# Reciprocal roots of the latents in pairs, and three weight splits moved from GpSimd to VectorE

## The chip, the cores and the metric

The kernel runs on one core of one Trainium2 chip, in one launch. The metric is the device time of one execution in microseconds (us); the median of several runs is given. The engines are PE (TensorE: matmuls and transposes), DVE (VectorE), ACT (ScalarE), POOL (GpSimd) and SP (SyncE, which here only issues DMAs).

## What is computed

Two transformer blocks in a row on 256 tokens of width 1024, all in fp32. The change touches the first half of the first block, cut here to the parts that matter:

```python
mod = silu(c) @ w_ada + b_ada                   # six vectors: sh1, sc1, gt1, sh2, sc2, gt2
h  = rmsnorm(x, g_norm1) * (1 + sc1) + sh1      # 256 x 1024
hc = rmsnorm(ctx, g_norm1) * (1 + scc1) + shc1  # the context, 256 x 1024
cq, ckv, kpe, rq, rk, rv, rg = split(h @ w_in)  # widths 256, 256, 32, 4 x 512
cq_c, ckv_c, kpe_c, ...      = split(hc @ w_in)
q   = rmsnorm(cq, g_q) @ w_uq                   # 8 heads of 64 + 32, rope on the 32
k,v = rmsnorm(ckv, g_kv) @ w_ukv                # 8 heads of 64 + 64; keys get kpe, with rope
# the same for ckv_c, kpe_c without rope; keys and values of both are joined
o_mla = softmax(q k^T / sqrt(96)) v             # 8 heads, 256 queries, 512 keys
o = concat(o_mla, retention(rq, rk, rv, rg)) @ w_out
x = x + gt1 * o
```

A convolutional feed-forward layer, and a second block with windowed attention, a gated recurrence, cross-attention and a feed-forward layer, follow. `rmsnorm(x, g)` is `x * (mean(x*x) + 1e-6) ** -0.5 * g` over a row. The *latents* are the 256-wide `cq` (query latents), `ckv` (key/value latents) and `ckv_c` (context latents), each in two tiles of 128 tokens.

## The kernel before, in words

Tokens lie on the 128 partitions, in two tiles. A product in fp32 is made of three products in the matmul format fp32r (`mm3`, line 185): each factor is split into a high part (a rounded copy) and a low part (the factor less its high part), and high x high, high x low and low x high are summed in PSUM. So each block of weights, 128 x 1024 of `raw` that a DMA brought, is split before use in `Weights.unit`: ACT casts the high part `wh` (line 222), and a subtraction makes the low part `wl` (line 225). Where a gain is folded in, lines 229 and 230 (ACT and DVE) do the same. Tiles of activations are transposed by PE against an identity matrix into a PSUM tile `tr` (line 167), and split on the way out: ACT casts the high part (line 159), DVE subtracts (line 160). There are two `tr` buffers.

Line 225 runs on DVE, except that before the end of the first half of the first block every third split after the sixteenth goes to POOL:

```python
GPU = 3
GPN = 16
eng = nc.gpsimd if GPU and self.ext is None and self.cnt % GPU == 0 and self.cnt > GPN else nc.vector
```

There are three such splits.

The program is written as Python generators; a scheduler then sets the order of each engine's instructions by their dependences, their modelled costs and some priorities. An engine runs its instructions strictly in the order that comes out, and an instruction that waits holds up all behind it.

The stages around the change, in the order of time:

- *ada ticks* (lines 544 and 547, DVE): the modulation vectors are summed up from 128 x 1024 blocks of `w_ada`, a block at a time, in between other work. When a vector is complete, `ada_done` multiplies it with a matrix of ones on PE, into `tr` tiles (lines 520 and 526); for `gt1` DVE adds the two halves to the bias (line 522) just before the latents begin, and until then both `tr` buffers are held.
- *Latents* (lines 612 to 676). One product gives `cq`, `ckv`, `kpe` and the context's `ckv`, `kpe` in PSUM tiles (`acc` and `at`). For each of the two query latents: ACT copies it to SBUF (line 636), ACT squares and sums it (`mean_sq`, line 143), POOL adds epsilon and raises to -0.5 (lines 640 and 641), and it is transposed and split. Its root `rq` is applied later, to the products with `w_uq` (line 695). Then, for each of the four key/value and context latents: ACT's square, POOL's root (`finish_rstd`, lines 138 and 139), ACT's scaled copy (line 663), transposition and split, and rope on the 32 columns of `kpe` (`rope32`, lines 650 to 656, DVE) or a copy of them (line 668). So POOL computes six roots, 128 x 1 each, query latents first. Products of a further projection (`strand_d`, line 185 into `acc`) fill PE's time beside it.
- *Weave* of attention and the remaining projections. For each half of the queries and each of eight heads `mla_half` has PE compute scores (line 742), DVE their maximum (745, 746), ACT the exponential with its sum (748), DVE the reciprocal and the normalisation (749, 750), PE four transposes (753), DVE or ACT the copy out of PSUM (758, 756), and PE the product with the values (764). Projections' products, weight splits and ada ticks lie in between.

Of the kernel before, what the change touches and what calls it, by code (L numbers as in the profile page):

```python
# [9 lines left out]
F32 = mybir.dt.float32  # L10
# [3 lines left out]
AF = mybir.ActivationFunctionType  # L14
# [10 lines left out]
EPS = 1e-6  # L25
# [5 lines left out]
MLA_ACT = (2, 5)  # L31
MOD = 'VVAVVAVA'
MID = 1
GPU = 3
GPN = 16
START = 'mmaamxXmaammaammaamaamaakmaaacaC'
NT2 = 5
NS1 = 4
# [51 lines left out]
def _body(nc, tc, A, out, es):  # L90
# [24 lines left out]
    def small(w=1, tag="sm", bufs=None):  # L115
        kw = {} if bufs is None else {"bufs": bufs}
        return sm.tile([P, w], F32, tag=f"{tag}{w}", name=f"{tag}{w}", **kw)
# [24 lines left out]
    def mean_sq(a, n, ss):  # L142
        nc.scalar.activation(junk[:, 0:a.shape[-1]], a, AF.Square, scale=n ** -0.5, accum_out=ss)  # L143
# [44 lines left out]
    class Weights:  # L188
        def __init__(self, pl, nraw, nsplit):
            self.base, self.nraw, self.nsplit = pl, nraw, nsplit  # L190
            self.ext, self.next, self.n = None, 0, 0
            self.cnt = 0

        def extend(self, pl, nsplit):
            self.ext, self.next, self.n = pl, nsplit, 0
# [20 lines left out]
        def unit(self, ap, nk, width, gains=None, raw=None):  # L216
            n = nk * width
            if raw is None:
                raw = self.load(ap, nk, n)
            wh, wl = self.pair()  # L220
            if gains is None:
                nc.scalar.copy(wh[:, 0:n], raw[:, 0:n])  # L222
                self.cnt += 1
                eng = nc.gpsimd if GPU and self.ext is None and self.cnt % GPU == 0 and self.cnt > GPN else nc.vector
                eng.tensor_tensor(out=wl[:, 0:n], in0=raw[:, 0:n], in1=wh[:, 0:n].bitcast(F32), op=ALU.subtract)  # L225
            else:
                for k in range(nk):
                    s = slice(k * width, (k + 1) * width)
                    nc.scalar.activation(wh[:, s], raw[:, s], AF.Copy, scale=gains[k])  # L229
                    nc.vector.scalar_tensor_tensor(out=wl[:, s], in0=raw[:, s], scalar=gains[k],  # L230
                                                   in1=wh[:, s].bitcast(F32), op0=ALU.mult,
                                                   op1=ALU.subtract)
            return wh, wl
# [62 lines left out]
    with ExitStack() as e1:  # L296
# [334 lines left out]
        ckT_l = S4((P, 2, 512), F32R)  # L631
        rq_rs = []
        kpe = s.tile([P, 4, 32], F32, name="kpe")
        for t in range(2):
            cq = S1()
            nc.scalar.copy(cq, aq[t][:, 0:256])
            r = small(1, "rq", 2)
            ss = small(1, "ss")
            mean_sq(aq[t][:, 0:256], 256, ss)
            nc.gpsimd.tensor_scalar(out=r, in0=ss, scalar1=EPS, scalar2=None, op0=ALU.add)  # L640
            nc.gpsimd.tensor_tensor(out=r, in0=r, in1=mhalf[:, 0:1], op=ALU.pow)
            rq_rs.append(r)
            transpose_split(cq, cqT_h[:, :, t * P:(t + 1) * P], cqT_l[:, :, t * P:(t + 1) * P], 2)

        def rope32(dst, src, t, nh):
            cb = C1("mcos")[:, t * 32:(t + 1) * 32]
# [11 lines left out]
        fill(1)  # L658
        for i in range(4):
            a = akv[i] if i < 2 else akc[i - 2]  # L660
            r = rms(a[:, 0:256], 256)
            ck = S1()
            nc.scalar.activation(ck, a[:, 0:256], AF.Copy, scale=r)
            transpose_split(ck, ckT_h[:, :, i * P:(i + 1) * P], ckT_l[:, :, i * P:(i + 1) * P], 2)
            if i < 2:
                rope32(kpe[:, i:i + 1, :], a[:, 256:288].unsqueeze(1), i, 1)
            else:
                nc.vector.tensor_copy(kpe[:, i, :], a[:, 256:288])
        tt = tr_tile()
        for i in range(4):  # L670
            nc.tensor.transpose(tt[0:32, i * P:(i + 1) * P], kpe[:, i, :], ident)
# [878 lines left out]
```

## Time and profile before

| | |
|---|---|
| median of 3 runs | 844.55 us (844.31 to 845.6) |
| the profiled execution | 847.59 us, of which 845.8 us are the span from its first to its last instruction |
| PE busy | 811.1 us, 96% of the span |
| DVE busy | 618.4 us, 73% |
| ACT busy | 481.4 us, 57% |
| POOL busy | 50.5 us, 6%, in 85 instructions |
| granted TensorE clock, mean | 0.991 of full speed |

The span is one execution as the profiler saw it. An engine's busy time counts the time in which it executes; waiting is idle time. The granted clock is given as a share of 2.4 GHz: 1.00 is that, 0.50 is 1.2 GHz. In rows of the timeline the first number is the start from the span's beginning, the second the duration, both in us; then come engine, line, operation, output and inputs by their names in the program, shapes and the number of instructions in the row. In brackets stands the idle time of the engine before it, and the instruction whose end is taken to have released it.

### The profile page before, as it was taken

Reading aid. Unit: us, or ns where it says so; the run is one execution under the profiler, and the core shown is the slowest. Engines: PE = TensorE matmul, PEld = TensorE weight load, DVE = VectorE, ACT = ScalarE, POOL = GpSimd, SP = SyncE. Lnnn points to the kernel's source line nnn. Section 1 sums busy time; section 2 is a strip of 40 time slices with the busy share of each in tenths; the row PEclk is TensorE's granted clock in tenths of the full one; section 3 lists DMA queues with packets and bytes.
Section 4 is the critical chain, followed back from the end, with each engine's and each line's share of the span. In section 5 each row is a group of like instructions: output and inputs, shape, how many; then the busy total and the mean of one; then the engine's idle time right before and its main releaser. Section 6 shows DMA issues by size and latency. Waiting matters only on the chain.

```text
span 845.8 us, 11966 instructions
## 1 busy us (share of the span) xinstructions
PE 811.1 (96%) x4368; PEld 657.4 (78%) x4368; DVE 618.4 (73%) x1036; ACT 481.4 (57%) x850; POOL 50.5 (6%) x85
## 2 busy tenths in 40 slices
PE   5989989999999999999999999999999999999996
PEld 4856968667687888888887777777788788888885
DVE  5638969995797698878778656875747787867743
ACT  7337354333565686656656656665626876757631
POOL 0000020110110200000000400001001100000000
PEclk9988999999999999999999999999999999999999
DMA  9796878853154566666564453433633686666501
GB/s 336 273 351 237 261 286 297 303 186 132 50 180 133 179 218 220 182 193 192 184 199 150 126 150 129 146 110 118 195 101 97 176 250 188 186 197 184 193 1 50
DMA packets 81531, 155.20 MB, mean 183 GB/s; under 512 B 5184, under 2 KB 43584, under 8 KB 81472
## 3 DMA queue, kind: packets, MB, share of 16 engines
q1 hardware_dynamic: 81472, 154.44, 56.7%
q8 instruction: 34, 0.56, 0.3%
q14 instruction: 25, 0.20, 0.1%
HBM read 152.85 MB, written 1.05 MB: 182 GB/s over the span
## 4 chain that ended last, share of the span: by engine, by line
PE 68%; ACT 2%; POOL 2%; DVE 1%; issue 1%; POOLq 0%; DVEq 0%; ACTq 0%
PE acc L185 34%; PE tr L255 9%; PE at L255 7%; PE tr L258 4%; PE at L258 3%; ACT junk L143 1%; PE at L1317 1%; PE at L1295 1%; PE tr L167 1%; PE tr L1236 1%; PE at L1186 1%; PE at L1188 1%; PE at L1266 0%; PE tr L764 0%; PE at L793 0%
## 5 line engine op out<-in xcount | busy, mean ns | idle before, releaser
L185 PE MATMUL acc<-wh,xT 128*128 128x512 f32 (+2 forms) x544 | 169.2, 388 | 1.8 <-ACT xT L159 1.8
L222 ACT CAST wh<-raw 128x1024 fp32r<-128x1024 f32 (+1 forms) x90 | 91.0, 1013 | 86.0 <-PE acc L185 30.5
L225 DVE TENSOR_TENSOR wl<-raw,wh 128x1024 fp32r<-128x1024 f32 (+1 forms) x87 | 103.5, 1192 | 36.9 <-ACT wh L222 36.7
L185 PEld LDWEIGHTS acc<-wh,xT 128*128 128x128 f32 x544 | 99.0, 189 | 24.6 <-issue 3.6
L225 DVE TENSOR_TENSOR xl<-raw,xh 128x1024 fp32r<-128x1024 f32 x68 | 82.6, 1220 | 29.2 <-ACT xh L222 28.5
L185 PE MATMUL acc<-wl,xT 128*128 128x512 f32 (+2 forms) x272 | 97.9, 386 | 0.0
L229 ACT ACTIVATE wh<-raw,fm 128x256 fp32r<-128x256 f32 (+3 forms) x128 | 70.3, 605 | 41.4 <-DMA raw<-in_wv_x_dram 13.7
L185 PE MATMUL acc<-xh,xT 128*128 128x512 f32 x288 | 92.9, 398 | 0.0
L222 ACT CAST xh<-raw 128x1024 fp32r<-128x1024 f32 x68 | 71.0, 1048 | 36.5 <-PE acc L185 12.8
L230 DVE SCALAR_TENSOR_TENSOR wl<-raw,fm,wh 128x256 fp32r<-128x256 f32 (+3 forms) x128 | 71.7, 609 | 15.9 <-ACT wh L229 15.7
L185 PEld LDWEIGHTS acc<-xh,xT 128*128 128x128 f32 x288 | 53.4, 188 | 11.7 <-issue 0.8
L255 PE MATMUL tr<-xT,wh 128*128 128x512 f32 x192 | 61.2, 398 | 0.0
L185 PEld LDWEIGHTS acc<-wl,xT 128*128 128x128 f32 x272 | 50.4, 190 | 10.0 <-issue 2.2
L185 PE MATMUL acc<-xl,xT 128*128 128x512 f32 x144 | 53.1, 395 | 0.0
L230 DVE SCALAR_TENSOR_TENSOR xl<-raw,fm,xh 128x256 fp32r<-128x256 f32 (+2 forms) x76 | 38.0, 550 | 12.7 <-ACT xh L229 12.7
L229 ACT ACTIVATE xh<-raw,fm 128x256 fp32r<-128x256 f32 (+2 forms) x76 | 37.7, 559 | 16.8 <-PE acc L185 8.1
L185 PE MATMUL acc<-xh,g 128*128 128x512 f32 x160 | 44.1, 389 | 0.0
L258 PEld LDWEIGHTS tr<-xT,wl 128*128 128x128 f32 x192 | 36.1, 188 | 7.9
L255 PE MATMUL at<-xT,xh 128*128 128x512 f32 x128 | 40.2, 395 | 0.0
L255 PE MATMUL at<-xT,wh 128*128 128x512 f32 x128 | 40.2, 395 | 0.0
L255 PE MATMUL tr<-xT,xh 128*128 128x512 f32 x128 | 40.2, 395 | 0.0
L258 PE MATMUL tr<-xT,wl 128*128 128x256 f32 x192 | 38.6, 278 | 0.0
(365 smaller groups left out, 1567.9 us busy)
## 6 DMA issues: line engine op xcount, KB each, us to landing
raw<-in_w_up_dram SPq DMA_DIRECT2D x66, 512.0 KB, 4.0
raw<-in_w_ada_dram SPq DMA_DIRECT2D x48, 512.0 KB, 5.6
raw<-in_w_down_dram SPq DMA_DIRECT2D x44, 512.0 KB, 4.3
raw<-in_w_in_dram SPq DMA_DIRECT2D x38, 512.0 KB, 4.3
raw<-in_w_gate_dram SPq DMA_DIRECT2D x22, 512.0 KB, 4.7
raw<-in_w_out_dram SPq DMA_DIRECT2D x16, 512.0 KB, 3.5
raw<-in_wk_x_dram SPq DMA_DIRECT2D x8, 512.0 KB, 5.8
raw<-in_wv_x_dram SPq DMA_DIRECT2D x8, 512.0 KB, 8.8
```

The source lines that it names most:

```text
L143: nc.scalar.activation(junk[:, 0:a.shape[-1]], a, AF.Square, scale=n ** -0.5, accum_out=ss)
L167: nc.tensor.transpose(t[:, j * P:(j + 1) * P], src[:, (b + j) * P:(b + j + 1) * P], ident)
L185: nc.tensor.matmul(accs[i], lhsT=xl if f == 2 else xh, rhs=wl[i] if f == 1 else wh[i], start=first and f == 0, stop=last and f == 2)
L222: nc.scalar.copy(wh[:, 0:n], raw[:, 0:n])
L225: eng.tensor_tensor(out=wl[:, 0:n], in0=raw[:, 0:n], in1=wh[:, 0:n].bitcast(F32), op=ALU.subtract)
L229: nc.scalar.activation(wh[:, s], raw[:, s], AF.Copy, scale=gains[k])
L230: nc.vector.scalar_tensor_tensor(out=wl[:, s], in0=raw[:, s], scalar=gains[k], in1=wh[:, s].bitcast(F32), op0=ALU.mult, op1=ALU.subtract)
L255: nc.tensor.matmul(a, lhsT=wh[:, o + b * P:o + (b + 1) * P], rhs=both, start=k == 0, stop=False, skip_group_check=True)
L258: nc.tensor.matmul(a[:, T:2 * T], lhsT=wl[:, o + b * P:o + (b + 1) * P], rhs=X.h[:, k, :], start=False, stop=k == 7, skip_group_check=True)
L1186: nc.tensor.matmul(o[cs, hs], lhsT=ATs[cs, cols], rhs=ih[cs, hs], start=True, stop=cg == 0)
L1188: nc.tensor.matmul(o[cs, hs], lhsT=qi[:, cols], rhs=Sst[cg - 1][:, hs], start=False, stop=True)
L1236: nc.tensor.matmul(sc[:, j * nk:(j + 1) * nk], lhsT=qTs[pr_, hd * P:(hd + 1) * P], rhs=kTs[pr_, 0:nk], start=True, stop=True)
```

## The change

It has two parts. All splits of weights go to DVE, the three of POOL among them. And the roots of the latents are taken two at a time: a pair's two mean squares are written to the columns of one 128 x 2 tile, and POOL takes both roots with one addition and one power. The pairs come in another order: the key/value pair, the context pair, and the query pair last, whose squares now read the SBUF copies of the query latents instead of PSUM. Two DVE copies put the query roots into a tile of their own. POOL's instructions become nine fewer (six small ones and three splits), DVE's five more (three splits and two copies).

```diff
--- before.py
+++ after.py
@@ -31,8 +31,6 @@
 MLA_ACT = (2, 5)
 MOD = 'VVAVVAVA'
 MID = 1
-GPU = 3
-GPN = 16
 START = 'mmaamxXmaammaammaamaamaakmaaacaC'
 NT2 = 5
 NS1 = 4
@@ -189,7 +187,6 @@
         def __init__(self, pl, nraw, nsplit):
             self.base, self.nraw, self.nsplit = pl, nraw, nsplit
             self.ext, self.next, self.n = None, 0, 0
-            self.cnt = 0
 
         def extend(self, pl, nsplit):
             self.ext, self.next, self.n = pl, nsplit, 0
@@ -220,9 +217,7 @@
             wh, wl = self.pair()
             if gains is None:
                 nc.scalar.copy(wh[:, 0:n], raw[:, 0:n])
-                self.cnt += 1
-                eng = nc.gpsimd if GPU and self.ext is None and self.cnt % GPU == 0 and self.cnt > GPN else nc.vector
-                eng.tensor_tensor(out=wl[:, 0:n], in0=raw[:, 0:n], in1=wh[:, 0:n].bitcast(F32), op=ALU.subtract)
+                nc.vector.tensor_tensor(out=wl[:, 0:n], in0=raw[:, 0:n], in1=wh[:, 0:n].bitcast(F32), op=ALU.subtract)
             else:
                 for k in range(nk):
                     s = slice(k * width, (k + 1) * width)
@@ -631,16 +626,19 @@
         ckT_l = S4((P, 2, 512), F32R)
         rq_rs = []
         kpe = s.tile([P, 4, 32], F32, name="kpe")
+        cqs = []
         for t in range(2):
             cq = S1()
             nc.scalar.copy(cq, aq[t][:, 0:256])
-            r = small(1, "rq", 2)
-            ss = small(1, "ss")
-            mean_sq(aq[t][:, 0:256], 256, ss)
-            nc.gpsimd.tensor_scalar(out=r, in0=ss, scalar1=EPS, scalar2=None, op0=ALU.add)
-            nc.gpsimd.tensor_tensor(out=r, in0=r, in1=mhalf[:, 0:1], op=ALU.pow)
-            rq_rs.append(r)
+            cqs.append(cq)
             transpose_split(cq, cqT_h[:, :, t * P:(t + 1) * P], cqT_l[:, :, t * P:(t + 1) * P], 2)
+
+        def rms_pair(a):
+            ss = small(2, "ss")
+            for i in range(2):
+                mean_sq(a[i], 256, ss[:, i:i + 1])
+            r = finish_rstd(ss, 2)
+            return [r[:, 0:1], r[:, 1:2]]
 
         def rope32(dst, src, t, nh):
             cb = C1("mcos")[:, t * 32:(t + 1) * 32]
@@ -658,14 +656,20 @@
         fill(1)
         for i in range(4):
             a = akv[i] if i < 2 else akc[i - 2]
-            r = rms(a[:, 0:256], 256)
+            if i % 2 == 0:
+                r = rms_pair([x[:, 0:256] for x in (akc if i else akv)])
             ck = S1()
-            nc.scalar.activation(ck, a[:, 0:256], AF.Copy, scale=r)
+            nc.scalar.activation(ck, a[:, 0:256], AF.Copy, scale=r[i % 2])
             transpose_split(ck, ckT_h[:, :, i * P:(i + 1) * P], ckT_l[:, :, i * P:(i + 1) * P], 2)
             if i < 2:
                 rope32(kpe[:, i:i + 1, :], a[:, 256:288].unsqueeze(1), i, 1)
             else:
                 nc.vector.tensor_copy(kpe[:, i, :], a[:, 256:288])
+        rq = rms_pair(cqs)
+        rqk = small(2, "rq", 1)
+        nc.vector.tensor_copy(rqk[:, 0:1], rq[0])
+        nc.vector.tensor_copy(rqk[:, 1:2], rq[1])
+        rq_rs += [rqk[:, 0:1], rqk[:, 1:2]]
         tt = tr_tile()
         for i in range(4):
             nc.tensor.transpose(tt[0:32, i * P:(i + 1) * P], kpe[:, i, :], ident)
```

How this moves instructions on the engines, at three places. The numbers at the names count the tiles of the program; those of the changed kernel are a few lower for the same tile, and its line numbers differ by 2 to 5.

The first is DVE's queue at the latents. `bc` is the sum for `gt1`, `acc_881` the first key/value latent, `s2_1109` the low part of the query latents' transposes (first `tr_1120`, second `tr_1132`; in the changed kernel `tr_1115` and `tr_1122`). Before:

```order
L522 TENSOR_TENSOR bc_764<-bc_764,tr_1102 128x512
L650 TENSOR_TENSOR s1k_1149<-acc_881,c1_91 128x32
L522 TENSOR_TENSOR bc_764<-bc_764,tr_1105 128x512
L160 TENSOR_TENSOR s2_1109<-tr_1120,s2_1108 128x2x128
L654 TENSOR_TENSOR s1k_1150<-acc_881,c1_91 128x2x8 x2
L656 TENSOR_TENSOR kpe_1112<-s1k_1149,s1k_1150 128x32
L160 TENSOR_TENSOR s2_1109<-tr_1132,s2_1108 128x2x128
```

Changed, with `rs2_1184` the root of the query pair:

```order
L517 TENSOR_TENSOR bc_764<-bc_764,tr_1102 128x512
L648 TENSOR_TENSOR s1k_1140<-acc_881,c1_91 128x32
L517 TENSOR_TENSOR bc_764<-bc_764,tr_1105 128x512
L652 TENSOR_TENSOR s1k_1141<-acc_881,c1_91 128x2x8
L158 TENSOR_TENSOR s2_1109<-tr_1115,s2_1108 128x2x128
L652 TENSOR_TENSOR s1k_1141<-acc_881,c1_91 128x2x8
L670 COPY rq2_1187<-rs2_1184 128x1
L671 COPY rq2_1187<-rs2_1184 128x1
L654 TENSOR_TENSOR kpe_1112<-s1k_1140,s1k_1141 128x32
L158 TENSOR_TENSOR s2_1109<-tr_1122,s2_1108 128x2x128
```

The rope product (650, now 648) stays ahead of the second bias add, and the two copies of the query roots now stand ahead of the split of the second query latent's transposes.

The second is DVE's queue in the weave, around the third pair of heads of the first half; `wl` are weights' low parts, `s2` probabilities, `g4` the ada sum. Before:

```order
L749 RECIPROCAL rc8_1430<-sums8_1429 128x1
L225 TENSOR_TENSOR wl_1953<-raw_1950,wh_1952 128x1024
L750 TENSOR_SCALAR s2_1673<-s2_1673,rc8_1430 128x512
L547 SCALAR_TENSOR_TENSOR g4_1905<-raw_1980,silc_92,g4_1905 128x1024
L758 COPY s2_1682<-tr_1677 128x512
L547 SCALAR_TENSOR_TENSOR g4_1905<-raw_1983,silc_92,g4_1905 128x1024
L749 RECIPROCAL rc8_1430<-sums8_1429 128x1
L547 SCALAR_TENSOR_TENSOR g4_1905<-raw_2100,silc_92,g4_1905 128x1024
L750 TENSOR_SCALAR s2_1689<-s2_1689,rc8_1430 128x512
```

Changed:

```order
L753 RECIPROCAL rc8_1421<-sums8_1420 128x1
L220 TENSOR_TENSOR wl_2076<-raw_2073,wh_2075 128x1024
L754 TENSOR_SCALAR s2_1664<-s2_1664,rc8_1421 128x512
L542 SCALAR_TENSOR_TENSOR g4_1896<-raw_2091,silc_92,g4_1896 128x1024
L749 TENSOR_REDUCE mx1_1789<-at_1787 128x1
L762 COPY s2_1673<-tr_1668 128x512
L750 TENSOR_SCALAR mx1_1789<-mx1_1789 128x1
L542 SCALAR_TENSOR_TENSOR g4_1896<-raw_2094,silc_92,g4_1896 128x1024
L753 RECIPROCAL rc8_1421<-sums8_1420 128x1
L220 TENSOR_TENSOR wl_2188<-raw_2185,wh_2187 128x1024
L754 TENSOR_SCALAR s2_1680<-s2_1680,rc8_1421 128x512
```

A split stood between a reciprocal and its normalisation once in these rows, and stands so twice now; from `wl_1944`, nine rows ahead of these, to `wl_2188` the changed queue has three splits, where the old one has one.

The third is the same pair of heads on ACT, and then on PE. ACT before:

```order
L748 ACTIVATE s2_1689,sums8_1429<-at_1684,mx1_1686 128x512
L222 CAST wh_2196<-raw_2194 128x1024
L756 COPY s2_1698<-tr_1693 128x512
L341 COPY s1k_1781<-tr_1776 128x256
```

ACT changed:

```order
L752 ACTIVATE s2_1664,sums8_1420<-at_1659,mx1_1661 128x512
L219 CAST wh_2187<-raw_2185 128x1024
L752 ACTIVATE s2_1680,sums8_1420<-at_1675,mx1_1677 128x512
L760 COPY s2_1689<-tr_1684 128x512
L752 ACTIVATE s2_1792,sums8_1420<-at_1787,mx1_1789 128x512
L336 COPY s1k_1772<-tr_1767 128x256
```

PE before:

```order
L753 MATMUL tr_1693<-ident_72,s2_1689 128x128 x4
L742 MATMUL at_1812<-s8_1207,s8_1210 128x512
L526 MATMUL tr_1776<-g4_1575,ones_70 32x256 x4
L764 MATMUL tr_1428<-s2_1698,s8_1337 64x128
```

PE changed:

```order
L757 MATMUL tr_1684<-ident_72,s2_1680 128x128 x4
L183 MATMUL acc_1693<-wh_1866,xT_804 128x512
L183 MATMUL acc_1693<-wl_1867,xT_804 128x512
L183 MATMUL acc_1693<-wh_1866,xT_804 128x512
L183 MATMUL acc_1694<-wh_1866,xT_804 128x512
L521 MATMUL tr_1767<-g4_1566,ones_70 32x256 x4
L768 MATMUL tr_1419<-s2_1689,s8_1328 64x128
```

On ACT the cast of the next weights now stands ahead of the exponential, no longer between it and the copy of the transposed probabilities (756, now 760); a further exponential stands ahead of the copy of the ada sum (341, now 336). On PE four products (line 183) now stand between the transposes (757) and the product with ones (521), where the scores of the next head stood (742).

## Rows read from the trace of the kernel before

**Rows 1.** The page: busy time of each engine, and the chain that ended last by engine.

```profile
PE 811.1 (96%) x4368; PEld 657.4 (78%) x4368; DVE 618.4 (73%) x1036; ACT 481.4 (57%) x850; POOL 50.5 (6%) x85
...
PE 68%; ACT 2%; POOL 2%; DVE 1%; issue 1%; POOLq 0%; DVEq 0%; ACTq 0%
```

**Rows 2.** Timeline of the latents, 114 to 121 us, all engines.

```profile
114.55 0.38 ACT L143 ACTIVATE junk<-acc 128x256 bf16<-128x256 f32 x1
...
115.10 0.38 ACT L143 ACTIVATE junk<-acc 128x256 bf16<-128x256 f32 x1
...
115.32 0.23 POOL L640 TENSOR_SCALAR rq<-ss 128x1 f32<-128x1 f32 x1
...
117.20 0.47 ACT L663 ACTIVATE s1k<-acc,rs 128x256 f32<-128x256 f32 x1 [1.63 <-POOL rs L139]
...
117.71 0.19 DVE L650 TENSOR_TENSOR s1k<-acc,c 128x32 f32<-128x32 f32 x1 [2.63 <-ACT s1k L663]
117.82 0.68 DVE L522 TENSOR_TENSOR bc<-bc,tr 128x512 f32<-128x512 f32 x1
...
118.45 0.36 ACT L159 CAST s<-tr 128x256 fp32r<-128x256 f32 x1
...
118.64 0.41 PE L167 MATMUL tr<-ident,s1k 128*128 128x128 f32 x2 [2.30 <-ACT junk L143]
...
118.84 0.42 DVE L160 TENSOR_TENSOR s<-tr,s 128x256 fp32r<-128x256 f32 x1 [0.35 <-ACT s L159]
...
120.30 0.63 PE L167 MATMUL tr<-ident,s1k 128*128 128x128 f32 x2
```

**Rows 3.** Windows: start:end, length, busy PE, PEld, DVE, ACT, POOL, clock, DMA share, GB/s.

```profile
120.36:123.66 3.30, 3.30 (x10) 2.58 (x9) 2.87 (x7) 1.86 (x4) 0.00 (x0) 0.50 0.36 94
...
120.00:160.00 40.00, 39.10 (x182) 31.31 (x181) 37.34 (x57) 19.19 (x33) 2.62 (x2) 0.96 0.79 263
160.00:200.00 40.00, 39.23 (x220) 26.62 (x220) 34.45 (x62) 10.54 (x22) 2.40 (x1) 1.00 0.67 229
```

**Rows 4.** Timeline of POOL, a 128x2 root before the latents.

```profile
62.99 0.66 POOL L138 TENSOR_SCALAR rs<-ss 128x2 f32<-128x2 f32 x1 [36.72 <-DVE ss L375]
63.74 0.71 POOL L139 TENSOR_TENSOR rs<-rs,mhalf 128x2 f32<-128x2 f32 x1
```

**Rows 5.** Timeline of POOL, its three splits.

```profile
154.04 2.54 POOL L225 TENSOR_TENSOR wl<-raw,wh 128x1024 fp32r<-128x1024 f32 x1 [33.95 <-ACT wh L222]
181.26 2.40 POOL L225 TENSOR_TENSOR wl<-raw,wh 128x1024 fp32r<-128x1024 f32 x1 [24.69 <-DVE g L547]
212.88 2.37 POOL L225 TENSOR_TENSOR wl<-raw,wh 128x1024 fp32r<-128x1024 f32 x1 [29.21 <-PE tr L753]
```

**Rows 6.** Timeline of DVE beside them, and like instructions without a POOL split.

```profile
154.89 2.77 DVE L225 TENSOR_TENSOR wl<-raw,wh 128x1024 fp32r<-128x1024 f32 x1
...
163.93 1.22 DVE L225 TENSOR_TENSOR wl<-raw,wh 128x1024 fp32r<-128x1024 f32 x1
...
179.96 1.28 DVE L547 SCALAR_TENSOR_TENSOR g<-raw,silc,g 128x1024 f32<-128x1024 f32 x1
...
182.46 2.28 DVE L547 SCALAR_TENSOR_TENSOR g<-raw,silc,g 128x1024 f32<-128x1024 f32 x1
...
214.33 1.20 DVE L750 TENSOR_SCALAR s<-s,rc 128x512 f32<-128x512 f32 x1
...
217.20 0.49 DVE L750 TENSOR_SCALAR s<-s,rc 128x512 f32<-128x512 f32 x1
```

**Rows 7.** Timeline of PE in the weave, its waits, and ACT's cast ahead of one.

```profile
159.36 0.66 PE L753 MATMUL tr<-ident,s 128*128 128x128 f32 x4 [0.90 <-DVE s L750]
...
187.61 1.04 ACT L222 CAST wh<-raw 128x1024 fp32r<-128x1024 f32 x1 [5.75 <-PE tr L753]
...
189.19 0.64 PE L526 MATMUL tr<-g,ones 128*32 128x256 f32 x8 [0.77 <-ACT s L756]
...
215.68 0.63 PE L753 MATMUL tr<-ident,s 128*128 128x128 f32 x4 [0.30 <-DVE s L750]
```

## Prediction

> **What bounds the kernel now.** I read the totals and the chain of waits first. TensorE (PE) is busy for 811.1 of 845.8 us, and 68% of the chain that ended last is PE [rows 1]. So work taken from GpSimd (POOL) or given to VectorE (DVE) counts only where PE waits for it. I then read the two stretches that the change touches: the timeline around the latents, and the weave of attention and projections behind them.
>
> Around the latents PE stands still [rows 2]. The transposes of the second query latent start at 118.64 after a wait of 2.30 us. The releaser named there, ScalarE's (ACT's) square at 115.10, had long been done. What ended last is on DVE: the second bias add at 117.82, which frees the transpose buffer. It stood in DVE's queue behind the rope product at 117.71, and that waited 2.63 us for ACT's scaled copy of the first key/value latent (117.20), which waited 1.63 us for POOL's root. So PE waits there for the root that comes third in POOL's queue.
>
> A second cost follows: from 120.36 to 123.66 the granted clock is 0.50, the lower of TensorE's two levels (1.2 GHz), right after PE stood largely idle [rows 3]. The 3.30 us of work in it would take 1.65 at the full clock.
>
> In the weave (150 to 290 us) PE waits little: 0.90 us for a normalisation, 0.77 for ACT's copy of transposed probabilities, 0.30 for another normalisation [rows 7].
>
> **Which time the sum is against.** The profiled execution took 847.59 us (span 845.8 and 1.79 around it), 3.04 above the median of 844.55. I work the sum on the trace and subtract it from the median. The 0.2% bound, about what a measurement of this kernel can tell from no change, is 1.69 us.
>
> **The roots in pairs.** Two query squares leave ACT's queue ahead of the key/value squares. One takes about 0.55 (114.55 to 115.10), so 1.10 is the most; since the second query copy now goes first, I take 0.9: the second key/value square starts near 114.2 and is read out by 114.8. A paired root takes POOL 0.66 and 0.71 on 128x2 after a long pause, 63.74 + 0.71 - 62.99 = 1.46 with the gap [rows 4]; it ends near 116.25. ACT then starts the scaled copy at 116.28 instead of 117.20, the rope product and the bias add follow, and PE starts the second query latent's transposes at 117.70 instead of 118.64: **0.94 us sooner**, the wait falling to 1.36.
>
> Little of that lasts. The root of the query latents is now the third pair. Its squares stand on ACT behind that scaled copy and the second context square. The context pair can start on POOL near 117.2 and takes some 1.05 (0.23 without a pause [rows 2], the gap, 0.71), the third pair as long: it ends near 119.4. Two one-column copies on DVE wait for it, and the split of the second query latent stands behind them, as DVE's order shows. With two copies of some 0.15 (the rope product, 32 columns wide, takes 0.19) and a split of 0.42 [rows 2] it ends near 120.15; only then is the buffer free for the second key/value latent's transposes. They start near 120.22, against 120.30 before. So the front's gain lies between -0.2 (the walk's 0.1 less 0.3 if the copies hold up more than it shows) and 0.94 (nothing is given back). I take 0.35, nearer the lower end, because the walk ends at 0.1, while products that move forward can keep some of the rest. This leaves the low clock as it was.
>
> The six instructions fewer on POOL are worth nothing by themselves: POOL is busy 50.5 us in all [rows 1]. The two DVE copies cost 0.3 us of DVE beside PE's products; the one thing they hold up is the split just told. Their cover gone, they would cost PE 0.3.
>
> **The splits.** POOL's three take 2.54, 2.40 and 2.37 us [rows 5]. Each lies over DVE work that is stretched [rows 6]: a split of 2.77 against 1.22, an ada step of 2.28 against 1.28, a normalisation of 1.20 against 0.49. That is 1.55 + 1.00 + 0.71 = 3.26 us of DVE. Done by DVE they cost 3 x 1.22 = 3.66. So DVE gets only 0.40 us more work, and what the change does is to move it.
>
> The Trainium skill ("Perfetto Trace Analysis", "Optimizing Scalar/DVE Operations") speaks against giving GpSimd's work to a saturated DVE: it says that unloading DVE onto GPSIMD can make sense, though it adds that the two share an SBUF read port, so that it might not help. By its first half the sum would carry 3.66 us of the busier engine; the rows agree with its second half, and the sum carries 0.40.
>
> Two of PE's waits hang on the stretched work: the split of 2.77 holds up the normalisation that PE waits 0.90 for, and the 1.20 normalisation is the one behind the 0.30. Both go: **1.20**. The third wait, 0.77 [rows 7], stands where ACT's cast of a weight, 1.04 us [rows 7], precedes the copy of the probabilities. In the new order ACT has no cast there, and PE has four products (0.18 each by 39.23 us for 220 instructions [rows 3], 0.7 in all) before it needs the copy's buffer. I count 0.45, leaving 0.3 for the exponential now ahead of ACT's next copy; the bounds are 0 and 0.77.
>
> Against it stands what three more splits in DVE's queue delay. In the new order a split of 1.22 stands between a reciprocal and its normalisation twice. The price of a delay is read from the first wait: 1.55 too late made PE wait 0.90, so 0.65 was slack there. A plain split would then cost 1.22 - 0.65 = 0.57. The bounds are 0 (slack of 1.22 or more) and 1.22 each. Of three I count one, **0.57**, since PE has between half a dozen and a dozen products before most of these transposes.
>
> **Sum.** 0.35 + 1.20 + 0.45 - 0.57 = 1.43 us. A profiled run like the one shown would take 846.16, the median 844.55 - 1.43 = **843.1**. Other transfers and the later stages have no part in the change; weights are split well before their use, so PE carries the gain through to the end.
>
> **Rivals.**
> - The clock does not fall. PE's pause is 0.94 shorter, and nowhere else from 160 to 200 does a wait of under one us lower the clock (1.00 there [rows 3]). Against: no row shows what a pause of 1.36 does. Of the 1.65 the renewed waits behind it leave about 1.15: 1.43 + 1.15 = 2.58, so 842.0. With the 0.94 kept whole besides and all 1.65 it would be 840.9. Chance 0.25.
> - Gains eaten by new waits. All three splits cost 0.57 instead of one: 843.1 + 1.14 = 844.3; without the front's 0.35, where the query root holds up as much as the key/value root gives, 844.6. That the new order simply does not bring forward what PE waits for belongs here. For: three DVE splits stand close in the new order, where one did. Chance 0.20.
> - Slower: DVE sets the pace between 160 and 200. DVE was busy 34.45 of 40 us there, 37.34 of 40 in the stretch before [rows 3], and that fuller stretch is where PE waited 0.90. If each added split delays a normalisation by its whole 1.22, PE pays 3.66 and keeps only 0.35 + 1.20: 844.55 + 2.11 = 846.7. It decides from the point at which the slack before the transposes (0.65 in the row above) is zero for all three. Against: PE was idle 0.77 in those 40 us, and none of it for DVE. Chance 0.13.
>
> **How the numbers follow.** My forecast has 0.40, with a range of its own of 842.0 to 844.2 (front -0.2 to 0.94, ACT's wait 0 to 0.77, zero to two new waits); something else, 0.02. Faster than 842.86: the clock rival's 0.25 and a little under half of the forecast, 0.18, make 0.43. Slower than 846.24: 0.13 and 0.01, 0.14. The rest, 0.43, lies within 0.2%. The range 841.2 to 845.9 leaves out the slower rival and the clock rival's far end, under 0.2 together.
>
> **What would show it.** In the changed profile: the second query latent's transposes near 117.7 with a wait near 1.4; the second key/value latent's near 120.2, with DVE's copies waiting for POOL until about 119.4 ahead of a split; a granted clock of 0.50 or 1.00 in 120 to 124; DVE rows of 2.77, 2.28 and 1.20 gone, 90 weight splits instead of 87 and DVE's busy time up by some 0.7 (0.40 and the copies); the PE waits of 0.90 and 0.30 gone. It is wrong if PE's wait before the second query latent stays above 2, if PE waits over 1 us in all for normalisations in the weave, or if the gain in time comes from a stage behind 290 us.

## The result and the profile after

The changed kernel took 841.32 us (median of 6 runs, 838.88 to 841.72), the kernel before 845.08 (6 runs in the same comparison, 843.68 to 851.11). The ratio is 0.9943, with a 95% interval from 0.9925 to 0.9961: 4.8 us faster (3.3 to 6.3), where 1.4 was forecast. The ratio is not that of the two medians, which are 3.8 us apart. A second comparison gave 0.9955 (0.9934 to 0.9976). The profiled execution took 841.72 us, its span 839.9, against 847.59 and 845.8 before. Of the page, the lines that answer to [rows 1]:

```profile
PE 809.9 (96%) x4368; PEld 657.2 (78%) x4368; DVE 618.2 (74%) x1041; ACT 481.2 (57%) x850; POOL 40.6 (5%) x76
...
PE 79%; ACT 2%; POOL 2%; DVE 1%; issue 1%; POOLq 0%; DVEq 0%; ACTq 0%
```

DVE's five more instructions left its busy time where it was. PE's two shares of the chain cannot be compared: all shares named add up to 74% of the span before and to 85% after, and the rest of the chain is not named in either.

Where the time went is read from four instructions of PE that both kernels have: the last product of the latents, the first transposes of the attention's queries, the first product of the retention, and the last product of all. The timeline of PE before (start, duration, line, operation):

```profile
112.48 0.30 PE L185 MATMUL at<-wh,xT 128*128 128x288 f32 x1
...
130.78 1.04 PE L701 MATMUL tr<-ident,g 128*96 128x128 f32 x8
...
226.92 0.70 PE L810 MATMUL at<-g,g 128*128 128x256 f32 x2
...
838.34 0.39 PE L185 MATMUL acc<-wh,g 128*128 128x512 f32 x1
```

and after, where lines are 2 lower or 4 higher:

```profile
110.09 0.30 PE L183 MATMUL at<-wh,xT 128*128 128x288 f32 x1
...
126.19 1.03 PE L705 MATMUL tr<-ident,g 128*96 128x128 f32 x8
...
219.86 0.70 PE L814 MATMUL at<-g,g 128*128 128x256 f32 x2
...
832.49 0.39 PE L183 MATMUL acc<-wh,g 128*128 128x512 f32 x1
```

At the first landmark the changed kernel is 2.4 us ahead. The change does not touch the stretch up to it: PE, DVE, ACT and POOL have the same instructions in the same order there in both kernels. That product ended at 112.78 in this profile of the kernel before, at 110.10 in a second one (below) and at 110.39 after, so the 2.4 us are scatter. In part they are the clock's. It is at 0.50 for a while in this stretch of every profile, for 10.24 us in this one, 3.41 in the second and 6.83 after (windows: start:end, length, busy time of PE, PEld, DVE, ACT and POOL, clock, DMA share, GB/s; the first line is before, the second after):

```profile
58.83:69.07 10.24, 8.29 (x27) 5.25 (x28) 7.10 (x14) 5.14 (x10) 1.38 (x2) 0.50 0.95 339
...
58.84:65.67 6.83, 6.36 (x22) 3.83 (x23) 4.09 (x9) 3.70 (x7) 1.38 (x2) 0.50 1.04 387
```

From the first landmark on the stages are compared, each from the end of the first landmark or the start of the next: **latents** 18.00 us before and 15.80 after, **weave** 96.14 and 93.67, **the rest** 611.81 and 613.02. Each stage holds the same matmuls in both kernels, in the rest also in the same order. So the two changed stages gained 2.2 and 2.5 us, and the rest gave 1.2 back.

The weave by windows, before:

```profile
130.78:226.92 96.14, 94.17 (x500) 66.94 (x498) 77.97 (x133) 36.49 (x70) 7.31 (x3) 1.00 0.60 208
```

and after:

```profile
126.19:219.86 93.67, 93.67 (x501) 67.23 (x499) 78.06 (x136) 36.40 (x70) 0.00 (x0) 1.00 0.62 213
```

PE was idle for 96.14 - 94.17 = 1.97 us before, exactly the three waits of [rows 7] (0.90 + 0.77 + 0.30), and is not idle at all after. Its busy time fell by another 0.50. DVE did three splits more in the same busy time, 78.06 against 77.97: what it now spends on them it had lost beside POOL's splits.

The latents after, from the timeline:

```profile
112.03 0.68 DVE L517 TENSOR_TENSOR bc<-bc,tr 128x512 f32<-128x512 f32 x1
...
112.37 0.22 POOL L136 TENSOR_SCALAR rs<-ss 128x2 f32<-128x2 f32 x1 [49.51 <-ACT junk L141]
...
112.67 0.71 POOL L137 TENSOR_TENSOR rs<-rs,mhalf 128x2 f32<-128x2 f32 x1
...
113.42 0.48 ACT L662 ACTIVATE s1k<-acc,rs 128x256 f32<-128x256 f32 x1 [0.58 <-POOL rs L137]
...
114.03 0.68 DVE L517 TENSOR_TENSOR bc<-bc,tr 128x512 f32<-128x512 f32 x1
...
114.86 0.41 PE L165 MATMUL tr<-ident,s1k 128*128 128x128 f32 x2 [0.89 <-ACT junk L141]
...
115.75 0.71 POOL L137 TENSOR_TENSOR rs<-rs,mhalf 128x2 f32<-128x2 f32 x1
...
116.50 0.15 DVE L670 COPY rq<-rs 128x1 f32<-128x1 f32 x1 [0.36 <-POOL rs L137]
...
116.73 0.42 DVE L158 TENSOR_TENSOR s<-tr,s 128x256 fp32r<-128x256 f32 x1
...
117.29 0.41 PE L165 MATMUL tr<-ident,s1k 128*128 128x128 f32 x2 [0.21 <-DVE s L158]
```

PE's wait before the second query latent's transposes (114.86) is 0.89 us instead of the 2.30 of [rows 2], and no low clock follows it: from 66 to 468 us the clock is 1.00. Two windows of the changed kernel, behind the latents and in the cross-attention, show where it fell instead:

```profile
120.36:123.66 3.30, 3.30 (x21) 2.88 (x20) 3.30 (x7) 1.48 (x3) 0.00 (x0) 1.00 0.61 196
...
468.34:471.55 3.21, 3.21 (x16) 3.21 (x16) 0.95 (x3) 1.80 (x4) 1.56 (x6) 0.52 0.02 6
```

The first has the times of the window of [rows 3] that had 0.50, and holds 21 matmuls where that held 10. The second is behind a wait of 1.25 us in a stage that the change doesn't touch; the kernel before has that wait too (1.27), and kept its clock. At half speed these 3.2 us can cost up to 1.6; the rest lost 1.2.

### The profile page after: what moved, and what is told of

Read it like the earlier page. It is cut to its first block, busy times and chain, and to the rows that moved or that the text cites. A ratio compares the mean times of both kernels' runs of the same rounds, so it can differ in the third digit from the quotient of the medians.

```text
span 839.9 us, 11960 instructions
## 1 busy us (share of the span) xinstructions
PE 809.9 (96%) x4368; PEld 657.2 (78%) x4368; DVE 618.2 (74%) x1041; ACT 481.2 (57%) x850; POOL 40.6 (5%) x76
## 4 chain that ended last, share of the span: by engine, by line
PE 79%; ACT 2%; POOL 2%; DVE 1%; issue 1%; POOLq 0%; DVEq 0%; ACTq 0%
PE acc L183 40%; PE tr L250 9%; PE at L250 7%; PE tr L253 4%; PE at L253 4%; PE at L746 2%; PE tr L768 1%; PE at L183 1%; ACT junk L141 1%; PE tr L165 1%; PE at L1321 1%; PE tr L757 1%; PE at L1299 1%; PE tr L1240 1%; PE at L718 1%
## 5 line engine op out<-in xcount | busy, mean ns | idle before, releaser
L220 DVE TENSOR_TENSOR wl<-raw,wh 128x1024 fp32r<-128x1024 f32 (+1 forms) x90 | 105.6, 1176 | 36.7 <-ACT wh L219 36.5
```

The source lines that it names most:

```text
L220: nc.vector.tensor_tensor(out=wl[:, 0:n], in0=raw[:, 0:n], in1=wh[:, 0:n].bitcast(F32), op=ALU.subtract)
```

## The experiments

The theory that the runs were to test: the two parts add up; the splits are worth what PE waited for them and for DVE's stretched work; the pairs are worth a shorter chain and the low clock that followed the long pause. The rivals: the prediction's own small terms, or the clock by chance.

All runs, with the three stages of each one's profile (us). "Low" says for how many us the granted clock was at 0.50 behind the pause at the latents and behind the cross-attention's wait. A run without a ratio is a single one. Up to query_first, and in eight_pool_splits, each stage holds the same matmuls in all profiles. In the runs with "gt1_late" or "squares" in their names five to nine matmuls changed places between the latents and the weave, so that these two columns can be compared only in their sum.

| run | median | ratio to before | latents | weave | rest | low, latents | low, cross-att. |
|---|---|---|---|---|---|---|---|
| before | | | 18.00 | 96.14 | 611.81 | 3.4 | - |
| before_look | 845.16 | | 17.96 | 96.49 | 611.78 | 3.4 | - |
| splits_only | 843.81 | 0.9978 (0.9962 to 0.9995) | 18.87 | 93.61 | 611.64 | 6.8 | - |
| pairs_only | 844.23 | 0.9973 (0.9957 to 0.9990) | 15.35 | 96.34 | 614.51 | - | 6.8 |
| changed | 841.32 | 0.9943 (0.9925 to 0.9961) | 15.80 | 93.67 | 613.02 | - | 3.4 |
| changed_again | 840.95 | 0.9955 (0.9934 to 0.9976) | 15.23 | 93.69 | 614.68 | - | 6.8 |
| no_copies | 841.29 | 0.9940 (0.9917 to 0.9963) | 14.98 | 93.65 | 613.50 | - | 3.4 |
| query_first | 841.03 | 0.9942 (0.9919 to 0.9965) | 15.30 | 94.08 | 611.53 | - | - |
| eight_pool_splits | 852.21 | 1.0074 (1.0049 to 1.0099) | 15.48 | 100.97 | 613.05 | - | 3.4 |
| gt1_late | 840.17 | 0.9941 (0.9918 to 0.9963) | 13.33 | 94.93 | 611.58 | - | - |
| gt1_late_no_copies | 842.04 | 0.9946 (0.9927 to 0.9965) | 14.29 | 95.42 | 611.66 | - | - |
| query_first_gt1_late | 842.82 | 0.9969 (0.9954 to 0.9985) | 15.67 | 94.83 | 611.75 | - | - |
| three_squares | 842.89 | | 17.55 | 92.26 | 612.02 | - | - |
| eight_squares | 844.11 | | 20.59 | 92.78 | 611.48 | - | - |

The clock was also recorded for every execution without a profile, as a mean over its span. If each microsecond at the lower level is counted as half lost, (1 - clock) x span is the time that the low clock took, and the rest of the span is what everything else took. (It is an upper bound for the clock's part, since in every profile 4 to 7 us of low clock lie at the end, behind the last product.) Means over the executions of one comparison:

| run | executions | span | mean clock | taken by the low clock | without it |
|---|---|---|---|---|---|
| before | 24 | 844.15 | 0.9928 | 6.05 | 838.09 |
| splits_only | 12 | 842.20 | 0.9920 | 6.74 | 835.46 |
| pairs_only | 12 | 842.11 | 0.9939 | 5.13 | 836.98 |
| changed_again | 7 | 840.11 | 0.9933 | 5.64 | 834.47 |

The six executions of the changed kernel in the first comparison have 839.00, 0.9945, 4.62 and 834.38.

### The two parts alone

splits_only is the kernel before with `GPU = 0`:

```diff
-GPU = 3
+GPU = 0
```

> The kernel before with its three GpSimd splits done by DVE, the roots as before. Theory 1 (the two parts add up; the splits are worth what PE waited in the weave): faster by 2.0 to 2.5 us, ratio 0.9970 to 0.9977; PE's waits of 0.90, 0.77 and 0.30 us for normalisations and the copy gone, and the front as before: the second query latent's transposes waiting 2.3 us and a granted clock of 0.50 behind them. Theory 2 (the prediction's terms: 1.20 + 0.45 - 0.57): faster by 1.1 us, 0.9987, with one new wait of about 0.6 for a normalisation. Theory 3 (the chip gained elsewhere, the splits are worth nothing): 1.000.

Ratio 0.9978, or 1.9 us (0.4 to 3.2). The waits of PE from 105 to 300 us (engine, line, releaser: us in all, times, longest):

```profile
PE tr L167 <- ACT junk L143: 2.3, 1, 2.3
PE tr L167 <- DVE bc L522: 0.7, 1, 0.7
PE tr L947 <- ACT g L929: 0.6, 1, 0.6
PE acc L185 <- ACT xT L159: 0.4, 1, 0.4
```

The three waits of the weave are gone and none has come, and the front's 2.3 stands; the 0.6 and 0.4 lie behind the weave. The weave shrank from 96.14 to 93.61. That is theory 1; theory 2's new wait is not there. Without the low clock's part the gain is 838.09 - 835.46 = 2.6 us.

This run changes more than the engine of three splits: the scheduler also puts some 20 of DVE's 132 instructions of the weave, and some 40 of PE's 499, in another order among the others. No run moves the splits and keeps the order, so what the new order alone is worth is not told apart.

pairs_only is the changed kernel with the three splits back on POOL:

```diff
+GPU = 3
+GPN = 16
...
+            self.cnt = 0
...
-                nc.vector.tensor_tensor(out=wl[:, 0:n], ...
+                self.cnt += 1
+                eng = nc.gpsimd if GPU and self.ext is None and self.cnt % GPU == 0 and self.cnt > GPN else nc.vector
+                eng.tensor_tensor(out=wl[:, 0:n], ...
```

> The changed kernel with the three GpSimd splits put back, the roots in pairs. Theory 1: the front gains 2.2 us, 0.6 by a shorter chain of waits and 1.6 because the granted clock stays at 1.00 behind the shorter pause: ratio 0.9974, the three stretched DVE instructions and the waits of 0.90 and 0.3 back. Theory 2 (the prediction's front term): faster by 0.35 us, 0.9996, the clock at 0.50 behind the pause. Theory 3 (whether the clock falls there is chance, not the pause): 0.6 us in the runs where it falls and 2.2 where not; the time scatters by 1.6 us.

Ratio 0.9973, 2.3 us (0.8 to 3.6). The latents took 15.35 us instead of 18.00, the clock staying up, and the weave 96.34, as before. Without the low clock's part the gain is 838.09 - 836.98 = 1.1 us. Its first POOL split, the DVE work beside it and PE's wait:

```profile
150.82 1.21 DVE L225 TENSOR_TENSOR wl<-raw,wh 128x1024 fp32r<-128x1024 f32 x1
...
151.03 3.25 POOL L225 TENSOR_TENSOR wl<-raw,wh 128x1024 fp32r<-128x1024 f32 x1 [33.99 <-ACT wh L222]
...
152.02 3.34 DVE L547 SCALAR_TENSOR_TENSOR g<-raw,silc,g 128x1024 f32<-128x1024 f32 x1
...
155.82 0.66 PE L762 MATMUL tr<-ident,s 128*128 128x128 f32 x4 [1.38 <-DVE s L759]
```

The DVE split ends at 152.03, POOL's split 2.25 later (154.28) and the ada step 1.08 after that (155.36): one after the other. An ada step of 1.28 takes 3.34 so, and PE waits 1.38 for the normalisation behind it. The two parts give 0.9978 x 0.9973 = 0.9951, between the two measurements of the whole:

> The changed kernel once more, for its interval and a second profile. Theory 1: the sum of the two parts, 4.2 to 4.7 us faster, 0.9944 to 0.9950, with the clock at 1.00 from 112 to 130 us. Theory 2 (the prediction): 0.9983. If the clock's fall is chance, this profile may show 0.50 behind the latents.

0.9955, and the clock at 1.00 behind the latents again. The parts add up, by the ratios within their intervals, and without the low clock's part more closely: 2.6 + 1.1 = 3.7 us beside 838.09 - 834.47 = 3.6.

### More splits on GpSimd

`GPU = 1` in pairs_only: all eight plain splits of the weave go to POOL.

> The changed kernel with all eight plain splits of the weave on GpSimd. If the two engines hold each other up there (as the three splits did, 2.5 us for three): 0.6 to 1 us lost for each, 5 to 8 us slower than the changed kernel, about 1.001 to 1.005 against the kernel before, with more stretched DVE rows. If GpSimd relieves DVE (8 x 1.22 us taken off it) and only an unlucky place cost time: the same as the changed kernel or faster, 0.994 to 0.995.

Ratio 1.0074, slower, and by more than the expectation had. The weave, by windows:

```profile
127.80:228.77 100.97, 94.52 (x501) 66.89 (x499) 79.76 (x128) 36.63 (x70) 20.21 (x8) 1.00 0.57 198
```

PE is idle for 6.45 us in it. The weave lost 100.97 - 93.67 = 7.30 us for eight splits, 0.91 each; pairs_only lost 96.34 - 93.67 = 2.67 for three, 0.89 each. DVE executes eight instructions fewer than after (128 against 136) and is busy for 1.7 us more. So POOL gave DVE no relief at all, at three places or at eight. Every profile with POOL splits has waits of PE in the weave (1.97, 2.25, 2.05 and 6.45 us in all), and in the others they come to 0.01 us at most. The whole kernel lost more than the weave, 850.48 - 840.11 = 10.4 us of mean span; 2.2 of that are the lower mean clock (0.9908).

### Pairing, order and the copies

no_copies hands the pair's columns to the products directly:

```diff
-        rqk = small(2, "rq", 1)
-        nc.vector.tensor_copy(rqk[:, 0:1], rq[0])
-        nc.vector.tensor_copy(rqk[:, 1:2], rq[1])
-        rq_rs += [rqk[:, 0:1], rqk[:, 1:2]]
+        rq_rs += rq
```

> The changed kernel without the two DVE copies of the query roots; the products' scaling reads the pair's tile itself, so that the split of the second query latent's transposes no longer waits on DVE for GpSimd's third root. If that wait still costs the front (the prediction's reason for giving most of the gain back): PE's waits of 0.47 and 0.21 us before the key/value transposes shrink and the kernel is 0.2 to 0.5 us faster than the changed one, 0.994 to 0.995 against the kernel before. If it doesn't: the same as the changed kernel, 0.995.

0.9940; its interval holds both results for the changed kernel. The latents took 14.98 us against 15.80 and 15.23, which is 0.25 and 0.8 less, where the changed kernel's two profiles differ by 0.57 themselves. So a cost of the copies is not shown, and it is some tenths at most.

query_first takes the query pair's roots ahead of the key/value pair's, from PSUM:

```diff
-        rq = rms_pair(cqs)
+        rq = rms_pair([x[:, 0:256] for x in aq])
```

with these lines moved ahead of the loop over the four latents.

> The changed kernel with the pairs in the old order: query pair first, then key/value, then context. It tells pairing from order. If the order carries the front's gain (the key/value root is what PE waits for): that root comes some 1.1 us later again, and the kernel loses 0.9 to 2 us against the changed one, 0.997 to 0.998. If pairing alone carries it: within 0.3 us of the changed kernel, 0.995. The scheduler puts the rope product behind both bias adds here, which would speak for the second.

0.9942, the same as the changed kernel: the order of the pairs was not what carried the gain. But this run did not isolate pairing as cleanly as meant. The scheduler put the rope product behind both bias adds, so the first query latent's transposes now wait for DVE, and the second's don't:

```profile
114.87 0.41 PE L165 MATMUL tr<-ident,s1k 128*128 128x128 f32 x2 [1.84 <-DVE bc L517]
```

What stands is that six roots in three pairs give the gain in either order, each with the order of instructions that the scheduler makes for it. No run keeps six single roots and takes the key/value roots first, so what pairing alone is worth stays open.

### The bias add

gt1_late moves gt1's products with ones and its additions behind the latents:

```diff
+        late = []
...
                 if k == 7:
-                    ada_done(g, ada_cur[g])
+                    if g == 2:
+                        late.append((g, ada_cur[g]))
+                    else:
+                        ada_done(g, ada_cur[g])
...
+        for x in late:
+            ada_done(*x)
         fill(4)
```

> The changed kernel with the products and additions for gt1 moved behind the latents, so that both transpose buffers are free when the latents begin and the second query latent's transposes don't wait for the second bias add behind the rope product. If that addition is what PE waits for: PE's waits of 0.75 and 0.89 us there go, part of it comes back as a longer wait for the first key/value latent's root; 0.5 to 1.0 us faster than the changed kernel, 0.993 to 0.994 against the kernel before. If the root alone sets the pace: within 0.2 us of the changed kernel.

0.9941. Of PE's waits at the latents one of 0.58 is left, but the products with ones, 1.88 us of PE, are in the weave now, and latents and weave together took 108.26 us against 109.47 and 108.92. The medians differ by less than the intervals; no gain is shown. Without the low clock's part the mean span is 833.33 (6 executions), 1.1 us under the changed kernel's, so the expectation may hold; the next run, which contains the same move, does not bear it out. Two combinations were no better:

> The changed kernel with gt1's products and additions behind the latents and without the two DVE copies. If PE's waits at the latents still cost time one by one: 0.5 to 1 us faster than the changed kernel, 0.993 to 0.994 against the kernel before. If the roots' chain sets the pace whatever is moved: the same as the changed kernel, 0.995.

0.9946: the same as the changed kernel, and without the low clock's part 834.96.

> The pairs in the old order (query pair first), and gt1's products and additions behind the latents. The two query latents are transposed at once and seven or more products lie ahead of the first key/value latent's transposes, so PE's pause at the latents should fall under 1 us. If pauses are what is left: 0.993 to 0.994, the best of all runs. If not: 0.995.

0.9969: worse, if anything. PE's waits at the latents are 1.14, 0.64 and 0.36 us; the pause did not fall under 1 us. So no version was found that beats the changed one beyond its interval.

### The clock behind the latents

before_look is a second profile of the kernel before.

> The kernel before once more, for a second profile of it. If the low clock behind the latents follows from the pause of 2.3 us: 0.50 there again for some 3 to 4 us. If it is chance: 1.00 there in this profile.

The pause and the clock behind it are there again, the wait in the timeline and the stretch by windows. The last line is the stretch in splits_only, where the clock stays down for longer:

```profile
115.89 0.41 PE L167 MATMUL tr<-ident,s1k 128*128 128x128 f32 x2 [2.29 <-ACT junk L143]
```

```profile
116.60:120.06 3.46, 3.46 (x11) 2.78 (x12) 2.84 (x12) 3.01 (x7) 0.65 (x2) 0.51 0.15 25
...
117.30:124.20 6.90, 5.86 (x17) 4.73 (x18) 5.29 (x16) 4.46 (x13) 2.15 (x5) 0.51 0.43 151
```

Two runs lengthen the changed kernel's pause by squares whose results nobody reads, three of them or, with `range(8)` and two buffers `sx`, eight:

```diff
         fill(1)
+        for t in range(3):
+            mean_sq(aq[t % 2][:, 0:256], 256, small(1, "sx", 3))
         for i in range(4):
```

> The changed kernel with three more squares of the query latents (unused results) ahead of the key/value squares on ACT, which puts the key/value root off by some 1.65 us. A longer pause of PE before the first key/value latent's transposes, 1 to 1.5 us by the order of PE. If only pauses of over 2 us bring the low clock there: 1.00 from 112 to 130 us. If chance does it: may be 0.50.

A pause of 1.60, the clock at 1.00 from 112 to 130. Both answers of the expectation allow that.

> The same with eight such squares, which puts the key/value root off by some 4.4 us; ten products of PE fill a part of it. A pause of 2 to 3.5 us before the first key/value latent's transposes. If the pause brings the low clock: 0.50 for 3 to 4 us behind it, and 1.7 us lost to it, beside the pause itself. If chance does it: may be 1.00.

The scheduler moved products into the gap and split it: waits of 1.26 and 1.59 with some 0.4 us of work between them, and the clock at 1.00 from 112 to 130. A single pause over 2 us did not come about, so neither answer of the expectation was put to the test. What the profiles show together: three of three with a pause of 2.3 us have the low clock behind the latents (before, before_look, splits_only), and none of eleven with pauses up to 1.84. That speaks for the pause as the cause at this place. But the length of one wait does not decide it. At 57 us, where the change has no part, all fourteen profiles have a pause of 1.68 to 2.69 us, and the clock falls to 0.50 in all of them (at 58.8 to 62.7). The shortest pause is that of eight_squares:

```profile
59.22 0.64 PE L331 MATMUL at<-raw,silc 128*32 128x256 f32 x8 [1.68 <-DMA raw<-in_w_ada_dram]
...
62.47:65.88 3.41, 3.40 (x9) 2.20 (x9) 2.39 (x5) 1.96 (x4) 0.33 (x1) 0.50 1.03 377
```

There 0.64 and 0.38 us of waiting follow before the clock falls. Yet 1.26 and 1.59 us with 0.4 of work between them, at the latents of the same profile, brought no low clock. What else decides stays open.

## Why the prediction was wrong

The direction and the order of the two parts were right, the size was a third of what came: 1.4 us against 3.8 (medians) to 4.8 (ratio). What failed are sizes of terms in the sum: the new wait (0.57) that did not come, the front's 0.35, which took most of its gain for given back, and the low clock, which was left as it was. Step by step:

**What bounds the kernel** held. PE was the bound, the time came from PE's waits, and POOL's and DVE's busy times (50.5 to 40.6 and 618.4 to 618.2 us) count for nothing by themselves.

**The front's term, 0.35, was mis-sized: the latents gained 2.2 to 2.8.** Three parts of its working are told apart by counting from the start of the products with ones (112.62 before, 110.22 after):
- The start of the key/value root was forecast at 114.8, 2.18 us on, and came 2.15 on. Right.
- Its price was not. The pair was costed at 1.46 us by a 0.66 of [rows 4], which I put down to POOL's long pause; it took 112.67 + 0.71 - 112.37 = 1.01, after just as long a pause (49.51). In the kernel before, a DVE split stands beside the slow addition, and another split on DVE (line 230, 62.82 to 63.58) beside the 0.66 of [rows 4]:

```profile
113.26 1.22 DVE L225 TENSOR_TENSOR wl<-raw,wh 128x1024 fp32r<-128x1024 f32 x1 [0.94 <-ACT wh L222]
...
113.96 0.61 POOL L640 TENSOR_SCALAR rq<-ss 128x1 f32<-128x1 f32 x1 [49.51 <-ACT junk L143]
```

POOL's addition ends at 114.57, 0.09 after the split. After the change it starts when that split is through, beside a bias add (112.03) one of whose inputs is in PSUM, and takes 0.22. In no_copies the addition of [rows 4] comes after 34.63 us of idling with no DVE instruction beside it, and takes 0.22 too:

```profile
61.26 0.22 POOL L136 TENSOR_SCALAR rs<-ss 128x2 f32<-128x2 f32 x1 [34.63 <-DVE ss L370]
```

So the pause was not the reason. With the shorter root the second query latent's transposes came 4.64 us on, where 5.08 was forecast and 6.02 was before.
- "Little of that lasts" failed. The second key/value latent's transposes came 7.07 us on; forecast was 7.60, before 7.68. The third root ended earlier than I had it (116.46, 6.24 us on, against 6.78), and no_copies shows that the copies behind it cost little. The chain kept 0.6 us at that point, not 0.1.

**The rival on the clock, with a chance of 0.25, was the case that came at the latents**, and I had priced it at 1.15: the low clock behind the latents cost 1.65 (3.30 at half speed), and all of it went. In the profile it was the largest item of the front. I had no row for a pause between 1 and 2.3 us and left the clock as it was; the low end of the range, 841.2, lies that far down only because of this rival. Over the whole kernel it is worth less, as told below.

**The weave's terms, 1.20 + 0.45 - 0.57 = 1.08, were mis-sized: it gained 2.5.** The 1.20 was right. ACT's wait went whole (0.77, not 0.45). The new wait of 0.57 did not come: the three splits took no more of DVE than the stretching that they replaced (78.06 against 77.97 us busy, where 0.40 more was forecast). And 0.50 came that had no term: PE's busy time fell with its three waits, some 0.17 for each; in the other profiles with POOL splits it is 0.14 to 0.21 for each wait, and the reason is not shown. The rows behind the 0.65 of slack and the 0.77 were one execution's: in before_look POOL's first split took 3.52 us, PE waited 1.42 for the normalisation behind it, and 0.53 where the row has 0.77.

**The rivals that ate the gain or slowed the kernel** did not come: no wait for a normalisation is left in the weave. The forecast's own range, 842.0 to 844.2, was narrower than the bounds in its bracket add up to (841.6 to 844.7).

What the forecast lacked altogether is the rest: 613.02 against 611.81, a low clock in the cross-attention. It fell there in five of the eleven profiles without the low clock behind the latents, and in none of the three with it. Whether the one follows from the other, or that is chance, stays open. With it the stages give 2.2 + 2.5 - 1.2 = 3.5 us, beside 3.8 by the medians. The means of all executions say how much the clock was worth in the end: the low clock took 6.05 us before and 5.64 or 4.62 after, so it gave 0.4 or 1.4 us, less than the 1.65 of the latents; with so few executions the figure is uncertain by more than half a microsecond. Everything else gave 3.6 or 3.7, splits_only 2.6 and pairs_only 1.1 of it. These two figures are the ones to hold against the forecast's 1.08 and 0.35.

## What to carry to other kernels

In this weave a split moved from DVE to GpSimd cost DVE as much as it took off it, and PE 0.9 us for each, at three or at eight; look at the DVE rows under a GpSimd row before counting it as free. Before a slow small GpSimd instruction is explained by what POOL did, look at what DVE does in those nanoseconds. Where a low clock follows a wait of TensorE in the trace, shortening the wait may win the clock's part too, and the sum should carry a share of it; but one profile shows the clock of one execution, so take its worth from the mean clocks of many, and compare the rest of the time without it.

## What the runs showed of the hardware

- Where DVE and POOL held each other up, nearly all the work of one came behind that of the other: a DVE split, POOL's split and an ada step, begun at 150.82, 151.03 and 152.02, ended at 152.03, 154.28 and 155.36 (pairs_only), and the ada step of 1.28 became 3.34. A small addition on POOL (128x1 or 128x2) takes 0.22 to 0.23 us alone, and 0.61 to 0.66 beside a DVE instruction with two large operands in SBUF that began 0.16 us or more before it, ending 0.07 to 0.09 us after that; where the two starts lie within 0.1 us it took 0.22 (before_look, gt1_late, eight_squares). Beside a DVE addition with one operand in PSUM it takes 0.22. In gt1_late and gt1_late_no_copies one took 0.64 beside a DVE instruction with one large operand in SBUF and a column (line 540). The Trainium skill ("SBUF — State Buffer", "SBUF: two separate sides") calls the port pair that the two share an exclusive lock, which a GpSimd operation, or a DVE one in a 2-port mode or with two SBUF inputs, holds for a whole instruction while the other blocks. The rows with two SBUF operands agree; whether line 540 ran in a 2-port mode no run here shows. In before_look POOL's split is recorded from 152.09 and a DVE split from 152.14, and it was DVE's that took its plain 1.22 us and POOL's that took 3.52, so the recorded starts did not tell which of them went ahead.
- A pause of 2.3 us of TensorE at the latents was followed by 3.4, 3.4 and 6.8 us at 0.50 in three of three profiles, pauses up to 1.84 at that place in none of eleven. Yet at 57 us, around pauses of 1.68 to 2.69, the clock fell in fourteen of fourteen, and behind one unchanged wait of about 1.25 us in the cross-attention it fell in five and not in nine.
